# Stick-breaking attention: a block's products are issued after the next block's turnings, with more operand tiles, and the last keys' values are added by GpSimd

## The chip, the cores and the metric

The kernel runs on one core of one Trainium2 chip. The metric is the device time of one execution in microseconds (us), as the median of several runs. The core has five engines that matter here: PE (TensorE, matmuls; PEld is its weight load), DVE (VectorE), ACT (ScalarE), POOL (GpSimd) and SP (SyncE, which issues nearly all DMA transfers). PSUM is the memory that PE writes to, SBUF the one for operands.

## The reference, cut to what matters

The reference is one step of a two-layer encoder, width 1024, 16 heads of 64, with 2048 prompt frames and 64 sample frames that follow 2048 cached ones. Layer 0 (mixer A) attends in a band of chunks with softmax, layer 1 (mixer B) with stick-breaking:

```python
def sb_block(q, k, v, q_pos, k_pos):
    z = jnp.einsum('bqhd,bkhd->bhqk', q, k).astype(jnp.float32) * SCALE
    mask = (k_pos[None, :] < q_pos[:, None])[None, None]
    log_fail = jnp.where(mask, jax.nn.log_sigmoid(-z), 0.0)
    later = jnp.flip(jnp.cumsum(jnp.flip(log_fail, -1), axis=-1), -1) - log_fail
    w = jnp.where(mask, jnp.exp(jax.nn.log_sigmoid(z) + later), 0.0)
    return jnp.einsum('bhqk,bkhd->bqhd', w.astype(v.dtype), v)
```

So the weight of a key is its own sigmoid times the product of (1 − sigmoid) of all keys between it and the query. Both mixers multiply their result by SiLU(gate), project it and add it to the stream. A last normalization follows.

The kernel uses another form of the sum over keys: with the stick that is left, s, after each key, the weights are differences of neighbouring s. The sum of weight times value is then a sum of s times the difference of neighbouring values, and at the end one term is left over per query tile, the value of the tile's last key. That term is what `last_values` and `ends` hold.

## The kernel before, in words

The work stands in stages: mixer A's projections (0 to 776 us in the trace), the band attention with its output projection (776 to 1452), mixer B's projections of keys, values, queries and gate (1454 to 2083), the stick-breaking attention (about 2100 to 3347), and the rest of its output projection with the last normalization (to the end). The scheduler of the tile framework orders each engine's instructions by a timeline of its own; the order in which the program issues them gives a priority only.

In the stick-breaking stage the loops run over pairs of heads `hp` (8), groups of 512 queries `g` (4), the head `h` in the pair (2) and chunks of 512 keys `c`, from the diagonal backwards. An item is one such chunk. `scores` (L467) makes z on PE, with q as the standing operand. `pass_sticks` turns z into sticks: ACT makes f = sigmoid (L1008), POOL multiplies neighbours, `two` (L1019), DVE runs the cumulative product, a scan (L1021, or L1011 on the diagonal), and POOL fills the other half, s (L1024). Then `weigh` (L483 to L509) takes one pack of four 128x128 squares of s: `flip` (L128) turns them on PE into the PSUM tile `wt`, `split` (L135 to L137) cuts them into two operands, a high half `ph` (ACT, L136) and a low half `pl` (DVE, L137), and two products per block add `vt` times each half into the PSUM tile `acc` (L499). `ph` and `pl` have four tiles each. `weigh_sample` (L511 to L558) does the same for the 64 sample frames, with narrower tiles `pp` (L538).

The left-over term is a matmul too. In mixer B's projections `stage_ends` (L357 to L364) reads the last row of each 128 values, splits it and writes it to DRAM, `v_end`. At the start of the attention this is loaded into `last_values`, and POOL builds a table `upto` of 17 rows of ones at the right tiles (17 `affine_select`, 17 casts). The first pack of each `acc` then issues, between its high and its low product, `acc <- upto, last_values` (L509, 64 of 128x512; L547, 16 of 128x64 for the sample).

When the last chunk is done, `gate_out` (L470 to L481) joins the two halves of `acc`: ACT copies one (L477), DVE adds the other (L478), and for the second head POOL multiplies by the gate (L480) and SP writes the result `o`.

`pipelined` (L700 on) runs the items with a lag of one: the scores of one item are issued interleaved with the weighing of the item before, and between them pieces of `filler`, projection jobs for the next queries and gates (`ps_j`, L601 to L603) and the output projection (`ps_o`). 54 `ps_j` matmuls stand before the first scores of the stick-breaking stage. Queries go to DRAM in eight writes per job (`q_b`, L166) and come back by `load_q` (L399), keys by L412, values by L419, gates by L405, all on SP's queue.

Of the kernel before, what the change touches and what calls it, by code (L numbers as in the profile page):

```python
# [16 lines left out]
P = 128  # L17
# [52 lines left out]
def encoder_step(ctx: ExitStack, tc: tile.TileContext, a: dict, o: dict):  # L70
# [41 lines left out]
    vend = dram.tile([len(TOK), H, P], F32R, name="v_end")  # L112

# [16 lines left out]
    banks = {}  # L130
# [226 lines left out]
    def stage_ends(half, pool, psum):  # L357
        cols, heads, n = slice(half * CH, half * CH + CH), slice(half * 8, half * 8 + 8), len(TOK)
        cur = pool.tile([P, CH], F32, name="vcur", tag="vr", bufs=2)
        nc.sync.dma_start(cur[: n - 1], vraw[1 : 1 + NP, cols].rearrange("(t p) c -> t p c", p=P)[:, P - 1])  # L360
        nc.sync.dma_start(cur[n - 1 : n], vraw[T : T + 1, cols])
        vs = pool.tile([P, 8, 2, DH], F32R, name="vs", tag="vs", bufs=2)
        split(vs[:n, :, 0, :], vs[:n, :, 1, :], cur[:n].rearrange("p (h d) -> p h d", d=DH))
        nc.sync.dma_start(f32(vend[:, heads]), f32(vs[:n]).rearrange("p h s d -> p h (s d)"))  # L364

# [106 lines left out]
    def gate_out(L, pool, acc, h, c0, n, gt, ot, hp, g):  # L472

        lo, up = slice(0, DH), slice(DH, P)
        mine, other = (lo, up) if h == 0 else (up, lo)
        tmp = pool.tile([P, CH], F32, name="otmp", tag="otmp", bufs=1)
        nc.scalar.activation(tmp[mine, :n], acc[other, c0 : c0 + n], AF.Copy)  # L477
        nc.vector.tensor_tensor(ot[mine, :n], acc[mine, c0 : c0 + n], tmp[mine, :n], ALU.add)  # L478
        if h == 1:
            nc.gpsimd.tensor_tensor(ot[:, :n], ot[:, :n], gt[:, :n], ALU.mult)  # L480
            nc.sync.dma_start(lay[L]["o"][g][hp], ot[:, :n])  # L481

    def weigh(pool, psum, acc, blocks, first, last, ends=None):  # L483
# [11 lines left out]
        for s, part in enumerate((ph, pl)):  # L495
            at = 0
            for i, (ws, v, c0) in enumerate(blocks):
                m = len(ws) * P
                last_mm[0] = mm(  # L499
                    acc[:, c0 : c0 + m],  # L500
                    v,
                    part[:, at : at + m],
                    start=(first and s == 0 and i == 0),
                    stop=(last and s == 1 and i == len(blocks) - 1),
                    skip_group_check=True,
                )
                at += m
            if ends and s == 0:
                mm(acc, *ends, start=False, stop=False, skip_group_check=True)  # L509

    def weigh_sample(pool, psum, total, blocks, first, ends=None):  # L511
# [13 lines left out]
        for f in flips:  # L525
            f()
        acc = psum.tile([P, CH], F32, name="acc", tag="acc", bufs=1)
        for i, pack in enumerate(packs):

            pp = pool.tile([P, 2, 2, 2, NS], F32R, name="pp", tag="ph", bufs=4)  # L530
# [5 lines left out]
            for j, (_, _, v, _) in enumerate(pack):  # L536
                for h in range(2):
# [8 lines left out]
                    if ends and i == 0 and j == 0:  # L546
                        mm(acc[:, h * P : h * P + NS], *ends[h], start=False, stop=False, skip_group_check=True)  # L547
# [154 lines left out]
    def pipelined(items, lag, filler, more, ready, later, lead):  # L702
# [49 lines left out]
        for two in late:  # L752
            run([], two)

# [29 lines left out]
    staged_b = [partial(stage_ends, i) for i in range(2)]  # L784
# [20 lines left out]
    with (  # L805
# [6 lines left out]
        banks.update(wt=3, fo="wt")  # L812
# [46 lines left out]
        def item(hp, g, h, q, gt, ot, bias, keys, vs):  # L859
# [28 lines left out]
            def weigh_pack(i):  # L888
                if i == 0:
                    st["acc"] = psum.tile([P, CH], F32, name="acc", tag="acc", bufs=1)  # L890
                last = i == len(packs) - 1
                weigh(lpool, psum, st["acc"], [block(j) for j in packs[i]], i == 0, last)
                if last:
                    gate_out("a", lpool, st["acc"], h, 0, CH, gt, ot, hp, g)
# [61 lines left out]
    with (  # L956
# [17 lines left out]
        nc.vector.tensor_copy(own, own_s)  # L974

        last_values = wpool.tile([P, H, P], F32R, name="last_values")
        upto = wpool.tile([P, T], F32R, name="upto")
        nc.gpsimd.memset(f32(last_values), 0.0)
        nc.sync.dma_start(f32(last_values[: len(TOK)]), f32(vend))
        ones = pool.tile([P, CH + 1], F32, name="ones", tag="s", bufs=11)[:, :P]  # L980
        nc.gpsimd.memset(ones, 1.0)
        for t, (r0, n) in enumerate(TOK):
            row = pool.tile([P, CH], F32, name="row", tag="f", bufs=3)[:, :P]
            nc.gpsimd.affine_select(
                out=row, in_=ones, pattern=[[0, P]], compare_op=ALU.is_equal, fill=0.0, base=-t, channel_multiplier=1,
            )
            nc.gpsimd.tensor_copy(upto[:, r0 : r0 + n], row[:, :n])
        KV, SB = 4, 11
        banks.update(wt=4, fo="wt")
# [41 lines left out]
        def items():  # L1031
            for part in ORDER:
                yield sum(16 * (4 * g + 3) for g in part)
                for hp in range(HP):
                    kv = {}
                    for g in part:
                        for h in range(2):
                            q = load_q("b", pool, hp, h, g * CH)
                            acc = psum.tile([P, CH], F32, name="acc", tag="acc", bufs=1)
                            carry = {}  # L1040
                            for c in range(g, -1, -1):
# [5 lines left out]
                                yield item(hp, g, h, q, gt, ot, kv[c], acc, carry, c)  # L1047
# [5 lines left out]
        def item(hp, g, h, q, gt, ot, kv, acc, carry, c):  # L1053
# [109 lines left out]
```

## Time and profile before

| what | value |
|---|---|
| median of 3 runs | 3462.01 us (3460.86 to 3463.1) |
| profiled execution | 3459.85 us |
| its span | 3458.1 us |
| PE busy | 3304.3 us (96%) |
| PEld busy | 2811.4 us (81%) |
| DVE busy | 1920.0 us (56%) |
| ACT busy | 1661.0 us (48%) |
| POOL busy | 1176.0 us (34%) |

The span runs from the first to the last instruction of the profile. A row of a group reads: line, engine, operation, output <- inputs, the tile (standing rows*columns, then partitions x elements), xcount | busy us, mean ns of one | idle time of its engine just before these instructions, and what ended most of it. A row of a timeline reads: start, duration, engine, line, operation, xcount, and in brackets the idle time before it with its releaser. Matmuls on PE overlap one another, so two durations in a row may add to more than the time that they take.

### The profile page before, as it was taken

What the parts mean: (1) busy time and instruction counts of PE and PEld (TensorE: products, weight loads), DVE (VectorE), ACT (ScalarE), POOL (GpSimd) and SP (SyncE); (2) the same over time, 40 slices, a digit from 0 to 9 for tenths busy, and PEclk for the clock granted to TensorE, in tenths of its full rate; (3) what the DMA queues carried; (4) which work ended last, traced back from release to release, by engine and by line L of the source; (5) the groups of instructions that cost most, each with busy time, mean ns of one, the idle gap of its engine ahead of it and who ended that gap; (6) DMA issues with size and microseconds to landing.
All of it is one profiled execution on the core that took longest, in us unless ns stands there. A gap on an engine that the chain in (4) does not pass through costs nothing.

```text
span 3458.1 us, 53876 instructions
## 1 busy us (share of the span) xinstructions
PE 3304.3 (96%) x18064; PEld 2811.4 (81%) x18064; DVE 1920.0 (56%) x3863; ACT 1661.0 (48%) x3609; POOL 1176.0 (34%) x1845
## 2 busy tenths in 40 slices
PE   8999999999999999999999997999999998999999
PEld 6788999987887998787888996777777776777777
DVE  4224422118988883220233325877778888877763
ACT  5223322228887772141233324655656666655641
POOL 2001210005553340020233002333466667667650
PEclk9999999999999999999999999999999999999999
DMA  6349998257788755443699678665534454334333
GB/s 191 133 163 325 340 307 263 93 189 247 240 281 249 242 188 165 131 145 111 203 320 324 222 204 240 185 194 176 174 97 126 142 175 150 121 102 139 123 101 110
DMA packets 463906, 659.85 MB, mean 191 GB/s; under 512 B 53017, under 2 KB 272185, under 8 KB 463613
## 3 DMA queue, kind: packets, MB, share of 16 engines
q1 hardware_dynamic: 454094, 630.46, 57.6%
q10 hardware_dynamic: 9536, 25.96, 2.0%
q8 instruction: 143, 2.34, 0.3%
q14 instruction: 133, 1.09, 0.1%
HBM read 387.94 MB, written 268.34 MB: 190 GB/s over the span
## 4 chain that ended last, share of the span: by engine, by line
PE 63%; DMA 11%; DVE 11%; ACT 4%; issue 4%; SPq 4%; POOL 2%; ACTq 0%; DVEq 0%; POOLq 0%
PE acc L499 8%; PE z L467 6%; PE wt L128 6%; PE ps_t L156 5%; PE ps_t L157 5%; PE ps_t L155 5%; PE ps_v L157 4%; PE ps_v L155 4%; PE ps_v L156 4%; PE ps_o L692 3%; PE ps_o L693 3%; PE ps_o L694 3%; DVE pl L137 3%; DVE s L1011 2%; DVE s L1021 2%
## 5 line engine op out<-in xcount | busy, mean ns | idle before, releaser
L128 PE MATMUL wt<-ident,s 128*128 128x128 f32 (+1 forms) x3472 | 555.0, 275 | 24.1 <-DVE pl L137 6.5
L137 DVE TENSOR_TENSOR pl<-wt,ph 128x512 fp32r<-128x512 f32 (+1 forms) x864 | 540.5, 654 | 66.0 <-ACT ph L136 63.8
L136 ACT ACTIVATE ph<-wt 128x512 fp32r<-128x512 f32 (+1 forms) x864 | 464.6, 583 | 112.5 <-PE wt L128 97.2
L128 PEld LDWEIGHTS wt<-ident,s 128*128 128x128 f32 (+1 forms) x3472 | 417.9, 141 | 116.8 <-DVE pl L137 13.0
L1008 ACT ACTIVATE f<-z 128x512 f32<-128x512 f32 (+4 forms) x680 | 354.2, 543 | 298.0 <-PE z L467 148.6
L1024 POOL TENSOR_TENSOR s<-f,s 128x256 f32<-128x256 f32 x416 | 366.0, 881 | 169.9 <-DVE s L1021 164.7
L499 PE MATMUL acc<-pl,vt 128*128 128x512 f32 (+3 forms) x1088 | 365.9, 370 | 33.6 <-DVE pl L137 31.8
L467 PE MATMUL z<-kt,q 128*128 128x512 f32 (+3 forms) x1280 | 386.3, 395 | 11.8 <-ACT f L1008 9.4
L155 PE MATMUL ps_t<-x_own,wh 128*128 128x362 f32 (+1 forms) x1152 | 381.6, 331 | 3.0 <-ACT wh L141 3.0
L156 PE MATMUL ps_t<-x_own,wh 128*128 128x362 f32 (+1 forms) x1152 | 378.5, 329 | 0.0
L157 PE MATMUL ps_t<-x_own,wl 128*128 128x362 f32 (+1 forms) x1152 | 377.8, 328 | 0.0
L499 PE MATMUL acc<-ph,vt 128*128 128x512 f32 (+3 forms) x1088 | 354.8, 360 | 6.3 <-ACT ph L136 3.8
L831 POOL TENSOR_SCALAR s<-s,rc 128x640 f32<-128x640 f32 (+5 forms) x264 | 194.3, 743 | 488.5 <-DMA vt<-v_a 246.0
L1021 DVE TENSOR_TENSOR_SCAN s<-two,s,own 128x256 f32<-128x256 f32 x384 | 279.8, 739 | 73.1 <-POOL two L1019 71.9
L1019 POOL TENSOR_TENSOR two<-f 128x256 f32<-128x256 f32 x416 | 259.1, 628 | 112.5 <-ACT f L1008 110.9
L499 PEld LDWEIGHTS acc<-pl,vt 128*128 128x128 f32 x1088 | 193.6, 190 | 82.5 <-DVE pl L137 66.3
L499 PEld LDWEIGHTS acc<-ph,vt 128*128 128x128 f32 x1088 | 201.6, 189 | 44.0 <-ACT ph L136 15.8
L467 PEld LDWEIGHTS z<-kt,q 128*128 128x128 f32 x1280 | 201.5, 190 | 44.1 <-ACT f L1008 28.5
L155 PEld LDWEIGHTS ps_t<-x_own,wh 128*128 128x128 f32 x1152 | 218.1, 189 | 4.5 <-ACT wh L141 3.6
L1011 DVE TENSOR_TENSOR_SCAN s<-f,own 128x128 f32<-128x128 f32 (+4 forms) x264 | 201.5, 789 | 35.3 <-ACT f L1008 34.4
L156 PEld LDWEIGHTS ps_t<-x_own,wh 128*128 128x128 f32 x1152 | 218.4, 190 | 0.9
L157 PEld LDWEIGHTS ps_t<-x_own,wl 128*128 128x128 f32 x1152 | 218.0, 189 | 0.3
(155 smaller groups left out, 6379.1 us busy)
## 6 DMA issues: line engine op xcount, KB each, us to landing
vt<-v_b SPq DMA_DIRECT2D x80, 512.0 KB, 5.9
v_b<-vs SPq DMA_DIRECT2D x64, 512.0 KB, 5.5
q<-q_a SPq DMA_DIRECT2D x64, 512.0 KB, 4.1
q<-q_b SPq DMA_DIRECT2D x64, 512.0 KB, 4.2
vt<-v_a SPq DMA_DIRECT2D x48, 512.0 KB, 6.4
kt<-k_b SPq DMA_DIRECT2D x48, 512.0 KB, 6.3
keys<-k_a SPq DMA_DIRECT2D x40, 512.0 KB, 6.3
v_a<-vs ACTq DMA_DIRECT2D x32, 512.0 KB, 2.7
```

Of the source, the lines that this page charges most:

```text
L128: nc.tensor.transpose(out, in_, ident[: in_.shape[0], : in_.shape[0]])
L136: nc.scalar.activation(hi, src, AF.Copy)
L137: nc.vector.tensor_tensor(lo, src, f32(hi), ALU.subtract)
L155: mm(out, sh(k), mh(k), start=(k == 0), stop=False)
L156: mm(out, sh(k), ml(k), start=False, stop=False)
L157: mm(out, sl(k), mh(k), start=False, stop=(k == NK - 1))
L467: mm(z, q[:, i, t * P : t * P + P], kt[:, h], start=(i == 0), stop=(stop and i == 1), skip_group_check=not stop,)
L499: last_mm[0] = mm(acc[:, c0 : c0 + m], v, part[:, at : at + m], start=(first and s == 0 and i == 0), stop=(last and s == 1 and i == len(bl ...
L1008: nc.scalar.activation(f[:, x0:], z, AF.Sigmoid, scale=-SCALE)
L1011: nc.vector.tensor_tensor_scan(pr[:, rev], f[:, rev], own[:, rev], 1.0 if carry_in is None else carry_in, ALU.mult, ALU.max if diag else A ...
L1021: nc.vector.tensor_tensor_scan(pr[:, CH - 2 :: -2], two[:, ::-1], own[:, : CH // 2], carry_in, ALU.mult, ALU.bypass)
L1024: nc.gpsimd.tensor_tensor(pr[:, 1:CH:2], by2[:, :, 1], pr[:, 2 : CH + 1 : 2], ALU.mult)
```

## The change

Four things are changed together.

1. `weigh` and `weigh_sample` don't issue a block's products at once. `weigh` puts them into a list `held`, and the next `weigh` (or `weigh_sample`, or the end of `pipelined`) issues them after its own turnings and split. `acc` is allocated when the first products are issued, and `gate_out` follows the last ones. This holds for both mixers.
2. `ph` and `pl` have six tiles each in mixer B (four in mixer A, as before).
3. The matmuls `acc <- upto, last_values` are gone, and with them `stage_ends`, `v_end`, `last_values` and the table `upto`.
4. In their place a tile `ends["b"]` holds the last values by head pair and query tile. It is made at the start of the stick-breaking stage: four loads of rows of `v_raw` (16 rows and one row for each half of the width), eight turnings `ps_e` on PE, and two copies on ACT. `gate_out` then adds it, broadcast over 128 queries, to `ot` on POOL before the multiplication by the gate (32 of 128x512, 8 of 128x64).

```diff
-    def stage_ends(half, pool, psum):
-        cols, heads, n = slice(half * CH, half * CH + CH), slice(half * 8, half * 8 + 8), len(TOK)
-        cur = pool.tile([P, CH], F32, name="vcur", tag="vr", bufs=2)
...
-        nc.sync.dma_start(f32(vend[:, heads]), f32(vs[:n]).rearrange("p h s d -> p h (s d)"))
...
         if h == 1:
+            if L == "b":
+
+                t0, m = g * (CH // P), max(n // P, 1)
+                by = ot[:, :n].rearrange("p (t q) -> p t q", t=m)
+                last = ends["b"][:, hp, t0 : t0 + m].unsqueeze(2).to_broadcast([P, m, n // m])
+                nc.gpsimd.tensor_tensor(by, by, last, ALU.add)
             nc.gpsimd.tensor_tensor(ot[:, :n], ot[:, :n], gt[:, :n], ALU.mult)
...
+    held = []
+
+    def release():
+
+        while held:
+            held.pop(0)()
...
-        ph = pool.tile([P, CH], F32R, name="ph", tag="ph", bufs=4)
-        pl = pool.tile([P, CH], F32R, name="pl", tag="pl", bufs=4)
+        ph = pool.tile([P, CH], F32R, name="ph", tag="ph", bufs=banks["ph"])
+        pl = pool.tile([P, CH], F32R, name="pl", tag="pl", bufs=banks["ph"])
         split(ph[:, :n], pl[:, :n], wt[:, :n])
...
-            if ends and s == 0:
-                mm(acc, *ends, start=False, stop=False, skip_group_check=True)
...
+        def products():
+            to = acc()
...
+            then()
+
+        release()
+        held.append(products)
...
-    staged_b = [partial(stage_ends, i) for i in range(2)]
+    staged_b = []
...
-        nc.sync.dma_start(f32(last_values[: len(TOK)]), f32(vend))
...
+        ends["b"] = wpool.tile([P, HP, len(TOK)], F32, name="ends")
+        for half in range(2):
+            cols, n = slice(half * CH, half * CH + CH), len(TOK)
+            cur = pool.tile([P, CH + 1], F32, name="vcur", tag="s", bufs=SB)
+            nc.sync.dma_start(cur[: n - 1, :CH], vraw[1 : 1 + NP, cols].rearrange("(t p) c -> t p c", p=P)[:, P - 1])
+            nc.sync.dma_start(cur[n - 1 : n, :CH], vraw[T : T + 1, cols])
+            ps = psum.tile([P, CH], F32, name="ps_e", tag="wt", bufs=banks["wt"])
+            for j in range(4):
+                flip(ps[:, j * P : j * P + n], cur[:n, j * P : j * P + P])
+            nc.scalar.activation(
+                ends["b"][:, 4 * half : 4 * half + 4], ps.rearrange("p (j q) -> p j q", j=4)[:, :, :n], AF.Copy
+            )
```

**PE, the fourth pair of heads.** This is PE's order of before in the middle of the attention; the number behind a name tells tiles apart, and `wt_23555` is the tile whose halves are `ph_23560` and `pl_23561`.

```order
L128 MATMUL wt_23555<-ident_66,s_23525 128x128
L128 MATMUL wt_23579<-ident_66,s_23525 128x128
L128 MATMUL wt_23597<-ident_66,s_23525 128x128
...
L467 MATMUL z_23618<-kt_23257,q_23542 128x512 x2
L467 MATMUL z_23644<-kt_23257,q_23641 128x128 x2
L499 MATMUL acc_23357<-ph_23560,vt_23259 128x512
L499 MATMUL acc_23357<-pl_23561,vt_23259 128x512
L499 MATMUL acc_23357<-ph_23584,vt_23259 128x512
L128 MATMUL wt_23658<-ident_66,s_23551 128x128
L128 MATMUL wt_23658<-ident_66,s_23575 128x128
L128 MATMUL wt_23658<-ident_66,s_23593 128x128
```

And the same place after; here `wt_23485` belongs to `ph_23490` and `pl_23491`.

```order
L126 MATMUL wt_23485<-ident_66,s_23454 128x128
L126 MATMUL wt_23509<-ident_66,s_23454 128x128
L126 MATMUL wt_23527<-ident_66,s_23454 128x128
...
L456 MATMUL z_23548<-kt_23191,q_23473 128x512 x2
L456 MATMUL z_23568<-kt_23191,q_23566 128x128 x2
L504 MATMUL acc_23442<-ph_23490,vt_23193 128x512
L504 MATMUL acc_23442<-pl_23491,vt_23193 128x512
L504 MATMUL acc_23442<-ph_23514,vt_23193 128x512
L126 MATMUL wt_23582<-ident_66,s_23481 128x128
L126 MATMUL wt_23582<-ident_66,s_23505 128x128
L126 MATMUL wt_23582<-ident_66,s_23523 128x128
```

Nothing moved here: in both, the other blocks' last turnings, four turnings of a further tile (left out) and four matmuls of scores stand between a block's last turning and its first product.

**SP, the start of the stick-breaking stage.** Before, the first loads of queries, keys and values stand ahead of the eight writes of the last query job (`q_b_115`).

```order
L588 DMA lraw<-in_w_in_b 128x8x128
L399 DMA q<-q_b_108 128x2x512
L412 DMA kt<-k_b_116 128x2x512
L419 DMA vt<-v_b 128x4x256
L166 DMA q_b_115<-sh 64x1088 x4
L166 DMA q_b_115<-sl 64x1088 x4
L405 DMA gt<-gate_b_125 128x512
```

After, three of the new loads of `v_raw` rows stand there, and the fourth with the first loads behind the writes.

```order
L594 DMA lraw<-in_w_in_b 128x8x128
L994 DMA vcur<-v_raw 16x512
L995 DMA vcur<-v_raw 1x512
L994 DMA vcur<-v_raw 16x512
L164 DMA q_b_115<-sh 64x1088 x4
L164 DMA q_b_115<-sl 64x1088 x4
L995 DMA vcur<-v_raw 1x512
L388 DMA q<-q_b_108 128x2x512
L401 DMA kt<-k_b_116 128x2x512
```

On PE the eight turnings `ps_e` stand right behind the last projection matmul and ahead of the first `ps_j`, so that PE's next work waits for the fourth load.

**POOL, around one `gate_out`.** Before, at one head pair's `gate_out` in the stick-breaking stage:

```order
L1019 TENSOR_TENSOR two<-f 128x256
L1020 COPY s<-s 128x1
L1024 TENSOR_TENSOR s<-f,s 128x256
L1019 TENSOR_TENSOR two<-f 128x256
L480 TENSOR_TENSOR ot<-ot,gt 128x512
L1019 TENSOR_TENSOR two<-f 128x256
L1024 TENSOR_TENSOR s<-f,s 128x256 x2
```

After, at the `gate_out` in the same place of the sequence:

```order
L1031 TENSOR_TENSOR two<-f 128x256
L1032 COPY s<-s 128x1
L1036 TENSOR_TENSOR s<-f,s 128x256
L1031 TENSOR_TENSOR two<-f 128x256
L474 TENSOR_TENSOR ot<-ot,ends 128x512
L1031 TENSOR_TENSOR two<-f 128x256
L1036 TENSOR_TENSOR s<-f,s 128x256
L475 TENSOR_TENSOR ot<-ot,gt 128x512
L1036 TENSOR_TENSOR s<-f,s 128x256
```

The add stands where the multiplication stood, and the multiplication two instructions of the stick chain later.

More of the change, by code (lines that the diff above doesn't have):

```diff
@@ L888, in weigh_pack, with acc, then @@
             def weigh_pack(i):
[L889 to L890 removed]
+                def acc():
+                    if i == 0:
+                        st["acc"] = psum.tile([P, CH], F32, name="acc", tag="acc", bufs=1)
+                    return st["acc"]
+                def then():
+                    if last:
+                        gate_out("a", lpool, st["acc"], h, 0, CH, gt, ot, hp, g)
                 last = i == len(packs) - 1
[L892 to L894 removed]
+                weigh(lpool, psum, acc, [block(j) for j in packs[i]], i == 0, last, then)
             return [partial(tile_of, t) for t in range(4)], [partial(weigh_pack, i) for i in range(len(packs))]
@@ L974, in encoder_step @@
         nc.vector.tensor_copy(own, own_s)
-        last_values = wpool.tile([P, H, P], F32R, name="last_values")
-        upto = wpool.tile([P, T], F32R, name="upto")
-        nc.gpsimd.memset(f32(last_values), 0.0)
-        nc.sync.dma_start(f32(last_values[: len(TOK)]), f32(vend))
[L980 to L985, printed above, removed]
-            )
-            nc.gpsimd.tensor_copy(upto[:, r0 : r0 + n], row[:, :n])
-        KV, SB = 4, 11
-        banks.update(wt=4, fo="wt")
+        KV, SB = 4, 11
+        banks.update(wt=4, fo="wt", ph=6)
+        ends["b"] = wpool.tile([P, HP, len(TOK)], F32, name="ends")
[9 more added lines that the diff above has]
+                ends["b"][:, 4 * half : 4 * half + 4], ps.rearrange("p (j q) -> p j q", j=4)[:, :, :n], AF.Copy
+            )
         new = Sample("b", wpool)
@@ L1051, in items, with item @@
                     ready.append(GROUPS)
-        def item(hp, g, h, q, gt, ot, kv, acc, carry, c):
+        def item(hp, g, h, q, gt, ot, kv, sums, carry, c):
             tiles = []
@@ L1072, in weigh_pack, with acc, then @@
                 first = c == g and i == 0
-                ends = (last_values[:, 2 * hp + h], upto[:, g * CH : g * CH + CH]) if first else None
-                weigh(lpool, psum, acc, [block(j) for j in packs[i]], first, last, ends)
-                if last:
-                    gate_out("b", lpool, acc, h, 0, CH, gt, ot, hp, g)
+                def acc():
+                    if first:
+                        sums["acc"] = psum.tile([P, CH], F32, name="acc", tag="acc", bufs=1)
+                    return sums["acc"]
+                def then():
+                    if last:
+                        gate_out("b", lpool, sums["acc"], h, 0, CH, gt, ot, hp, g)
+                weigh(lpool, psum, acc, [block(j) for j in packs[i]], first, last, then)
             return [partial(tile_of, t) for t in range(4)], [partial(weigh_pack, i) for i in range(len(packs))]
@@ L1105, in two @@
             def two():
-                ends = [(last_values[:, 2 * hp + h], upto[:, NP:T]) for h in range(2)]
-                weigh_sample(lpool, psum, totals[hp], blocks, cs[0] == 4, ends if cs[0] == 4 else None)
+                weigh_sample(lpool, psum, totals[hp], blocks, cs[0] == 4)
                 if cs[-1] == 0:
```

49 lines of the change are left out of this document (21 added, 28 removed).

## The prediction

> **What bounds the kernel now.** I read the head of the page first, then the table of windows, then the groups of instructions by line, and last the timelines of the places that the change touches. The page's head gives the span and each engine's busy time:
>
> ```profile
> span 3458.1 us, 53876 instructions
> PE 3304.3 (96%) x18064; PEld 2811.4 (81%) x18064; DVE 1920.0 (56%) x3863; ACT 1661.0 (48%) x3609; POOL 1176.0 (34%) x1845
> ```
>
> TensorE (PE) is the bound on the average: 3458.1 − 3304.3 = 154 us is all that it idles. An average over stages isn't enough, so here are four windows of 100 us: the end of mixer B's projections, then the stick-breaking stage early, in the middle and late. The columns after the width are PE, PEld, DVE, ACT and POOL busy with their counts, then the granted clock, DMA share and GB/s.
>
> ```profile
> 2000.00:2100.00 100.00, 80.31 (x482) 79.23 (x480) 26.31 (x78) 24.05 (x75) 5.08 (x12) 0.92 0.78 216
> 2200.00:2300.00 100.00, 94.25 (x537) 78.41 (x535) 79.06 (x143) 58.34 (x135) 36.83 (x62) 1.00 0.65 189
> 2900.00:3000.00 100.00, 94.21 (x505) 72.64 (x503) 78.11 (x127) 58.81 (x120) 66.24 (x121) 1.00 0.40 126
> 3200.00:3300.00 100.00, 96.57 (x541) 77.46 (x540) 81.29 (x131) 62.73 (x126) 69.75 (x126) 1.00 0.40 127
> ```
>
> In the stick-breaking stage PE works 94 to 97% of the time, DVE about 80% and POOL up to 70%. So a matmul taken out there is worth nearly its own time, and PE's waits are worth at most 3 to 6%. Only one window shows a large hole, the first; I come to it below. Which waits does the hold aim at? The groups of the turning (L128), the split (L137) and the products (L499), with idle time before them and what ended it:
>
> ```profile
> L128 PE MATMUL wt<-ident,s 128*128 128x128 f32 x3456 | 552.3, 275 | 23.7 <-DVE pl L137 6.5 <-POOL s L1024 4.9 <-DVE pp L137 3.1
> L499 PE MATMUL acc<-pl,vt 128*128 128x512 f32 (+3 forms) x1088 | 365.9, 370 | 33.6 <-DVE pl L137 31.8
> L499 PEld LDWEIGHTS acc<-pl,vt 128*128 128x128 f32 x1088 | 193.6, 190 | 82.5 <-DVE pl L137 66.3
> ```
>
> Products wait 33.6 us on PE itself for the low half `pl`, and its weight load waits 66.3 us, of which most lies beside other matmuls. So the most that a perfect hold could bring is between 32 and 66 us.
>
> **The change, part by part.** *The matmuls removed.* Here are all 64 plus 16 instructions, and a place of each kind in PE's timeline.
>
> ```profile
> L509 PE MATMUL acc<-upto,last_values x64: 388/392/403, 2127.3 to 3333.2; 128*128 128x512 f32 x64
> L547 PE MATMUL acc<-upto,last_values x16: 297/297/298, 2170.5 to 2493.6; 128*128 128x64 f32 x16
> ```
>
> ```profile
> 2607.01 0.48 PE L499 MATMUL acc<-ph,vt 128*128 128x512 f32 x1
> 2607.32 0.39 PE L509 MATMUL acc<-upto,last_values 128*128 128x512 f32 x1
> 2607.55 0.40 PE L499 MATMUL acc<-pl,vt 128*128 128x512 f32 x1
> ```
>
> ```profile
> 2170.28 0.33 PE L538 MATMUL acc<-pp,vt 64*128 64x128 f32 x1 [0.26 <-DVE ot L478]
> 2170.53 0.30 PE L547 MATMUL acc<-upto,last_values 128*128 128x64 f32 x1
> 2170.76 0.32 PE L538 MATMUL acc<-pp,vt 64*128 64x128 f32 x1
> 2171.02 0.30 PE L547 MATMUL acc<-upto,last_values 128*128 128x64 f32 x1
> 2171.15 1.09 PE L538 MATMUL acc<-pp,vt 128*128 128x128 f32 x8
> ```
>
> Matmuls overlap, so the price is start to start and not the duration: 2607.55 − 2607.32 = 0.23 us for the wide one, 64 × 0.23 = 14.7 us. The narrow ones stand between products of the sample: from 2170.28 to 2171.15 two products and two of ours take 0.87 us; two products of 1.09 / 8 = 0.14 us alone would take 0.27, so ours cost 0.60 / 2 = 0.30 us, or up to 0.32 us where the weight loads bind; I take 0.32: 16 × 0.32 = 5.1 us. Together 19.8 us of PE time, on an engine that is 94 to 97% busy there. If PE instead waits in their place, part of it isn't seen: lower bound half, 10 us.
>
> *The hold.* As written, a block's products are issued after the next block's turnings. But the scheduler decides the order on PE, and the order of before has that already: between a block's turnings and its products there stand scores and products of others. The two orders, laid beside each other in the section on the change, show the same sequence at the same place. Over the 648 packs of the stick-breaking stage, the work on PE between the last turning and the first product, with each matmul at the trace's start-to-start time, has a median of 3618 ns before and 3450 ns after; in most packs that lose distance it is one removed matmul's. Where such a product does wait, distance isn't the reason:
>
> ```profile
> 2283.18 0.45 PE L499 MATMUL acc<-ph,vt 128*128 128x512 f32 x1
> 2285.11 0.50 PE L499 MATMUL acc<-pl,vt 128*128 128x512 f32 x1 [1.49 <-DVE pl L137]
> ```
>
> ```profile
> 2282.96 1.52 DVE L1011 TENSOR_TENSOR_SCAN s<-f,own 128x256 f32<-128x256 f32 x2
> 2284.40 2.45 DVE L137 TENSOR_TENSOR pl<-wt,ph 128x512 fp32r<-128x512 f32 x4
> ```
>
> DVE had two scans of 1.52 us ahead of the `pl` that PE wanted. Neither a hold nor six operand tiles in place of four shorten DVE's own queue. I cost the hold, the extra tiles and the small reordering together at 0, between −10 (a third of the 32 us) and +10 (giving each pack the mean wait that packs at its distance have in the trace, an estimate, the waits of products rise from 76 to 83 us).
>
> *The start of the stick-breaking stage.* The stage that made `v_end` in mixer B's projections is gone; in its place four loads of rows of `v_raw` and eight turnings `ps_e` stand between the last projection matmul and the first `ps_j`. That is the hole of the first window. PE, then SyncE's queue (SPq), then the landing of a 32 KB load of the same kind:
>
> ```profile
> 2083.03 0.32 PE L157 MATMUL ps_t<-x_own,wl 128*128 128x362 f32 x1
> 2100.54 0.79 PE L601 MATMUL ps_j<-big,lwh 128*128 128x512 f32 x1 [17.19 <-DVE sl L137]
> ```
>
> ```profile
> 2092.80 0.94 SPq L588 DMA_DIRECT2D lraw<-in_w_in_b  x1
> 2093.84 1.43 SPq L399 DMA_DIRECT2D q<-q_b  x1
> 2099.61 3.58 SPq L166 DMA_DIRECT2D q_b<-sh  x4
> 2103.29 3.84 SPq L166 DMA_DIRECT2D q_b<-sl  x4
> ```
>
> ```profile
> vcur<-v_raw SPq DMA_DIRECT2D x2, 32.0 KB, 2.0
> ```
>
> In the new order three of the four loads go out before the eight writes of `q_b`, and the fourth (one row) behind them. The writes end at 2103.29 + 3.84 = 2107.1; the load issues in about 0.4 us, lands some 2.0 us later at 2109.5, and after four turnings at the clock of an idle PE `ps_j` starts at 2110.5, not at 2100.54: +10 us. The first loads of q, keys and values move from 2093.84 to behind 2107.5, still before the 54 `ps_j` matmuls are through, and two waits at the stage's start, which were on loads, should shrink, since PE comes later and the loads come only some 3 us later:
>
> ```profile
> 2123.44 1.22 PE L467 MATMUL z<-kt,q 128*128 128x512 f32 x4 [2.61 <-ACT f L1008]
> 2138.73 0.41 PE L467 MATMUL z<-kt,q 128*128 128x128 f32 x2 [0.91 <-DMA q<-q_b]
> ```
>
> (ACT is named for the first; the chain of waits has a key load there.) They give back about 3 us. Net +7 us, bounds +4 (the last row lands faster) and +11 (nothing given back).
>
> *The adds on POOL.* 32 of 128x512 and 8 of 128x64, in front of the multiplication by the gate. The first row is the nearest, the same kind of operation on the same tile; then come VectorE's sum of two halves, and the stick chain's scan and `two`:
>
> ```profile
> L480 POOL TENSOR_TENSOR ot<-ot,gt 128x512 f32<-128x512 f32 x64 | 82.7, 1292 | 133.4 <-DVE ot L478 124.4 <-DMA gt<-gate_a 8.9
> L478 DVE TENSOR_TENSOR ot<-acc,otmp 64x512 f32<-64x512 f32 x128 | 87.7, 685 | 68.5 <-ACT otmp L477 66.6
> L1021 DVE TENSOR_TENSOR_SCAN s<-two,s,own 128x256 f32<-128x256 f32 x384 | 279.8, 739 | 73.1 <-POOL two L1019 71.9
> L1019 POOL TENSOR_TENSOR two<-f 128x256 f32<-128x256 f32 x416 | 259.1, 628 | 112.5 <-ACT f L1008 110.9
> ```
>
> 32 × 1.29 = 41 us of POOL time, on an engine with 30 to 60% of its time free in this stage. Behind an add on POOL stand the next `two` and `s` of the stick chain, and DVE's scans wait for `two`; PE itself waited on POOL's `s` for 4.9 us only (the L128 row above). One block's scores are a whole item ahead of its products, which covers a delay of 1.3 us in most places. Bounds 0 and 41 us; nearest is the 4.9 us over 416 `s`, so I take +3, range 0 to 8. The 17 selections and 17 casts of the removed table stood on POOL where it is 5% busy (first window): 0.
>
> A rule of the Trainium skill speaks against this part: GPSIMD Engine Reference, section 4.1, gives elementwise sums of two tiles to VectorE, with GpSimd about twice as slow. The trace agrees (1292 ns here; VectorE's sum of half the partitions at L478 has a mean of 685 ns), and by VectorE the sum would be 32 × 0.69 = 22 us on the engine that is already late for `pl`. So row and rule lead apart, and POOL, which PE rarely waits for, is the cheaper place here.
>
> *Mixer B's projections.* Two `stage_ends` with six DMAs go from SyncE's queue, where the first row stood ahead of PE's first wait there, the second row:
>
> ```profile
> 1669.81 7.48 SPq L344 DMA_DIRECT2D vcur<-v_raw  x2
> 1695.24 0.93 PE L128 MATMUL ps_n<-ident,kf 128*128 128x128 f32 x4 [2.17 <-ACT kn L386]
> ```
>
> Of these 2.17 us and the smaller waits behind them I take −2, bounds −4 and +4 (another order on the queue can also cost a wait of this size). Mixer A keeps its instructions and four tiles, and its order changes slightly: 0, in the ±10 above.
>
> *The sum.* −19.8 + 0 + 7 + 3 − 2 = −11.8, rounded to −11 for what PE's remaining waits take up. The profiled execution took 3459.85 us (span 3458.1 and 1.75 around it), so it would take about 3449; the median of the runs is 2.2 us higher, 3462.01, and the forecast for the median is **3451 us**.
>
> **The rivals.**
>
> *The hold does what it says.* If products really wait behind more work, most of the `pl` waits go: 32 to 66 us, say 40, so 3451 − 40 = 3411 us. For it: `pl` is the largest releaser of PE. Against it: the order on PE barely moves, and DVE, 80% busy, is what is late. Chance 0.10.
>
> *Nothing is left of it.* The removed matmuls only filled waits (half of 19.8 = 10 us remains), the start costs 10 or 11 and POOL 0 to 8: −10 + 10 + 3 − 2 = +1 at one end, and −4 with 5 of the start given back: 3458 to 3463 us. For it: POOL and DVE both show gaps that PE's order doesn't control. Against it: PE at 94 to 97%. Chance 0.23.
>
> *POOL becomes late, slower.* If each add stands just before a `two` or `s` for which scan, flips and so PE wait, all 41 us come onto the path: 3451 − 3 + 41 = 3489 us. It decides from about 15 us, when the adds eat the 19.8 + 2 − 7 of the other terms, and from 22 us it can be measured. For it: DVE idles 71.9 us on `two`, and POOL works 66 to 70% late in the stage. Against it: PE's own 4.9 us on `s`. Chance 0.07.
>
> The same end could be reached by another way, a block of VectorE by GpSimd. These rows are DVE's subtractions between 2199 and 3300 us, min/median/max in ns:
>
> ```profile
> L137 DVE TENSOR_TENSOR pl<-wt,ph x516: 398/679/694, 2199.6 to 3299.0; 128x512 fp32r<-128x512 f32 x155, 128x256 fp32r<-128x256 f32 x17
> L137 DVE TENSOR_TENSOR big<-woraw,big x16: 656/693/1371, 2831.7 to 2911.1; 128x512 fp32r<-128x512 f32 x16
> ```
>
> `pl`, with one operand in PSUM, never took over 694 ns in 516; `big`, with both in SBUF, took up to 1371. Only such subtractions would be hit by the adds, and they are few: under 1 us in all. The Trainium skill, SBUF — State Buffer, in "SBUF: two separate sides", says that VectorE with two SBUF inputs and GpSimd lock a port pair against each other; the trace agrees in these two rows.
>
> **How the numbers follow.** Forecast 0.60, nothing left 0.23, hold works 0.10, POOL late 0.07. A measurement of this kernel can tell about 0.2%, or 6.9 us: faster is under 3455.1, slower over 3468.9. The forecast's own range is 3443 to 3459 (the bounds −10 and +10 taken less than fully, with the others), of which about a fifth lies over 3455: faster 0.48 + 0.10 + 0.03 of the second case = 0.61; same 0.12 + 0.19 = 0.31; slower 0.07 + 0.01 = 0.08. The range reaches from 3440 (nearly the lower bound of the reordering) to 3463 (the second case), and leaves out the hold's and POOL's cases, 0.17.
>
> **What would show it.** PE's busy time falls by 64 × 0.39 + 16 × 0.30 = 30 us as the page counts it; the groups L509 and L547 are gone. The idle time before products for `pl` stays between 25 and 40 us; under 15 would prove the hold right and me wrong. From the last projection matmul to the first `ps_j` it is 17.5 us before (2100.54 − 2083.03) and should be 26 to 29; under 21 would prove the start's term wrong. The add takes about 1.29 us each, and the flips' wait on POOL's `s` stays under 13 us; 30 or more would be the slower rival.

## The result and the profile after

The changed kernel takes 3477.63 us in the median of 4 runs (3473.66 to 3482.18), the kernel before in the same comparison 3461.44 us (4 runs, 3457.29 to 3463.1). The ratio is 1.0054 with a 95% interval from 1.0040 to 1.0067: 18.7 us slower, where 3451 us and a range to 3463 had been forecast. The profiled execution took 3478.49 us with a span of 3476.7 us. Below, a difference between two runs is the difference of their ratios to the kernel before, times 3460 us; a ratio's interval is about ±0.001, so a single difference carries some ±5 us.

The head of the page after, and its groups of turnings, products and scans:

```profile
span 3476.7 us, 53697 instructions
PE 3291.9 (95%) x17992; PEld 2800.0 (81%) x17992; DVE 1922.3 (55%) x3861; ACT 1655.6 (48%) x3609; POOL 1200.7 (35%) x1849
```

```profile
L126 PE MATMUL wt<-ident,s 128*128 128x128 f32 x3456 | 559.8, 276 | 36.3 <-POOL s L1036 10.3 <-DVE pp L135 6.7 <-DVE s L1023 4.4
L504 PE MATMUL acc<-pl,vt 128*128 128x512 f32 (+3 forms) x1088 | 366.4, 370 | 42.2 <-DVE pl L135 39.7
L474 POOL TENSOR_TENSOR ot<-ot,ends 128x512 f32<-128x512 f32 x32 | 33.4, 1043 | 85.0 <-DVE ot L467 84.8
L1033 DVE TENSOR_TENSOR_SCAN s<-two,s,own 128x256 f32<-128x256 f32 x384 | 280.4, 738 | 94.6 <-POOL two L1031 93.3
```

PE is busy for 12 us less and the span is 18.6 us longer: PE idles 185 us, not 154. Its waits before the `pl` products didn't go with the hold, they rose from 33.6 us to 42.2; the waits before turnings rose from 23.7 to 36.3 us, and DVE's scans wait 93.3 us for POOL's `two`, where it was 71.9. PE's busy time isn't a pure count of work: the same 17,992 matmuls of the changed kernel and its variants were busy for 3280.3 us in the trace with the highest mean granted clock (0.994, run `early_six_tiles`) and for 3294.1 us in one at 0.990 (`early_ends`). The changed kernel's trace has 0.989, that of the kernel before 0.991. How much of a difference in time is a difference in clock, no run separates.

The windows of 1210 us inside the stick-breaking stage show the same from PE's side, the kernel before first and the changed one second:

```profile
2130.00:3340.00 1210.00, 1148.99 (x6322) 921.00 (x6320) 972.35 (x1623) 739.14 (x1563) 706.03 (x1276) 1.00 0.48 145
```

```profile
2130.00:3340.00 1210.00, 1128.09 (x6208) 899.92 (x6206) 964.92 (x1615) 730.53 (x1557) 733.01 (x1301) 1.00 0.48 145
```

PE idles 1210 − 1148.99 = 61.0 us before and 81.9 us after. The windows stand at fixed times, while the stage begins later after the change, so here are the same two traces cut at events: the last projection matmul, the stage's first scores, and the last product.

| part | before, us | PE idle | after, us | PE idle |
|---|---|---|---|---|
| all before the last projection matmul | 2083.0 | 63.2 | 2084.0 | 62.9 |
| to the first scores | 32.0 | 17.2 | 44.4 | 28.1 |
| first scores to last product | 1245.1 | 65.4 | 1244.5 | 85.9 |
| behind the last product | 98.0 | 8.1 | 103.8 | 7.9 |

The stick-breaking stage is as long as before, although 80 matmuls are gone from it: what was taken from PE there came back as waiting. The start costs 12.4 us, and the work behind the last product takes 5.8 us more. Ahead of the stage little changes in sum, but two parts of it do: from its first scores to its last product mixer A's band attention takes 4.6 us more (536.2 and 540.8), and mixer B's projections take 4.5 us less (632.0 and 627.5).

The start of the stage, on PE and on SP's queue:

```profile
2083.99 0.32 PE L155 MATMUL ps_t<-x_own,wl 128*128 128x362 f32 x1
2102.77 0.58 PE L126 MATMUL ps_e<-ident,vcur 17*128 17x17 f32 x4 [18.45 <-DVE sl L135]
2113.00 0.58 PE L126 MATMUL ps_e<-ident,vcur 17*128 17x17 f32 x4 [9.65 <-DMA vcur<-v_raw]
2113.50 0.79 PE L607 MATMUL ps_j<-big,lwh 128*128 128x512 f32 x1
```

```profile
2097.59 0.30 SPq L994 DMA_DIRECT2D vcur<-v_raw  x1
2101.80 3.11 SPq L164 DMA_DIRECT2D q_b<-sh  x4
2105.01 4.35 SPq L164 DMA_DIRECT2D q_b<-sl  x4
2109.40 1.19 SPq L995 DMA_DIRECT2D vcur<-v_raw  x1
```

This is the chain that the prediction described: the fourth load is issued behind the eight writes, PE's second four turnings wait 9.65 us for it, and the first `ps_j` comes 2113.50 − 2083.99 = 29.5 us after the last projection matmul. The two waits of 2.61 and 0.91 us that the prediction expected to shrink are gone from the start of the stage.

### The profile page after: what moved, and what is told of

It reads as the page before. It is cut to its first block, busy times and chain, and to the rows that moved or that the text cites. A ratio compares the mean times of both kernels' runs of the same rounds, so it can differ in the third digit from the quotient of the medians.

```text
span 3476.7 us, 53697 instructions
## 1 busy us (share of the span) xinstructions
PE 3291.9 (95%) x17992; PEld 2800.0 (81%) x17992; DVE 1922.3 (55%) x3861; ACT 1655.6 (48%) x3609; POOL 1200.7 (35%) x1849
## 4 chain that ended last, share of the span: by engine, by line
PE 46%; DVE 13%; DMA 6%; issue 4%; ACT 4%; POOL 3%; SPq 2%; ACTq 0%; DVEq 0%; POOLq 0%
PE acc L504 7%; PE z L456 6%; PE wt L126 5%; DVE pl L135 4%; PE ps_o L698 3%; PE ps_o L699 3%; PE ps_o L700 3%; DVE s L1023 3%; DVE s L1033 3%; PE ps_v L153 2%; PE ps_v L155 2%; PE ps_v L154 2%; PE ps_j L607 2%; PE ps_t L154 2%; PE ps_t L155 2%
## 5 line engine op out<-in xcount | busy, mean ns | idle before, releaser
L126 PE MATMUL wt<-ident,s 128*128 128x128 f32 (+1 forms) x3472 | 562.8, 276 | 36.3 <-POOL s L1036 10.3
L504 PE MATMUL acc<-pl,vt 128*128 128x512 f32 (+3 forms) x1088 | 366.4, 370 | 42.2 <-DVE pl L135 39.7
L456 PE MATMUL z<-kt,q 128*128 128x512 f32 (+3 forms) x1280 | 384.7, 395 | 14.5 <-ACT f L1020 12.6
L1033 DVE TENSOR_TENSOR_SCAN s<-two,s,own 128x256 f32<-128x256 f32 x384 | 280.4, 738 | 94.6 <-POOL two L1031 93.3
L504 PEld LDWEIGHTS acc<-pl,vt 128*128 128x128 f32 x1088 | 193.7, 190 | 89.3 <-DVE pl L135 73.4
L504 PEld LDWEIGHTS acc<-ph,vt 128*128 128x128 f32 x1088 | 201.5, 190 | 44.4 <-ACT ph L134 15.5
L349 POOL TENSOR_TENSOR vprev<-vprev,vcur 128x512 f32<-128x512 f32 (+1 forms) x66 | 86.7, 1313 | 410.3 <-DMA vprev<-in_cache_b_v 150.7
```

What stands on the lines that cost most here:

```text
L126: nc.tensor.transpose(out, in_, ident[: in_.shape[0], : in_.shape[0]])
L456: mm(z, q[:, i, t * P : t * P + P], kt[:, h], start=(i == 0), stop=(stop and i == 1), skip_group_check=not stop,)
L504: last_mm[0] = mm(to[:, c0 : c0 + m], v, part[:, at : at + m], start=(first and s == 0 and i == 0), stop=(last and s == 1 and i == len(blo ...
L1033: nc.vector.tensor_tensor_scan(pr[:, CH - 2 :: -2], two[:, ::-1], own[:, : CH // 2], carry_in, ALU.mult, ALU.bypass)
```

## The experiments

All runs were made in five rounds beside the kernel before, each round on another chip; so runs are compared by their ratios. Three theories were set against each other: the hold costs; the adds on POOL cost; the changed order of instructions gives changes of any sign.

**The parts undone one at a time.** First the hold:

```diff
-        release()
-        held.append(products)
+        products()
```

> The changed kernel with the hold undone: each block's products are issued right behind its own turnings and split, everything else as changed (six tiles, adds on POOL, new start). If the hold costs, by the trace after: mixer A's band took 685 us after against 679 before (6 us), and PE's waits in the stick-breaking stage grew by some 20 us, of which the hold would have half. Theory 'hold' expects 10 to 16 us less than the changed kernel (ratio to before about 1.001 to 1.003). Theory 'POOL' expects only the 6 us of mixer A (ratio about 1.004). A rival, that any rearrangement of the order gives changes of this size, expects no rule: either sign, up to 10 us.

Measured: 3468.82 us, ratio 1.0033 (1.0021 to 1.0045). 7 us less than the changed kernel: below the 10 to 16 that 'hold' expected, close to the 6 that 'POOL' allowed, and not outside the rival of either sign up to 10 us. This run alone doesn't tell the theories apart.

The hold alone was put into the kernel before (the list `held` and the late `acc`, with the matmuls of the last values inside the held products).

> The kernel before with the hold alone, four tiles, its matmuls of the last values kept inside the held products. Theory 'hold' expects 10 to 16 us more than before (3471 to 3477, ratio 1.003 to 1.005), 6 of it in mixer A's band. Theory 'POOL' expects no more than those 6 us (ratio up to 1.002).

Measured: 3462.72 us, ratio 1.0011 (1.0001 to 1.0021), 4 us. Less than 'hold' expected, and within what 'POOL' allowed. In its trace the stick-breaking stage, cut at events as above, was no longer than before (1243.4 and 1245.1 us), and the band attention was (540.6 and 536.2 us).

The changed kernel without the adds:

```diff
-                nc.gpsimd.tensor_tensor(by, by, last, ALU.add)
```

> The changed kernel without the 40 adds on POOL; the last keys' values are left out of mixer B's result, the tile for them is still made. Theory 'POOL': DVE's wait on POOL's two rose from 78 to 97 us and PE's wait on POOL's s from 4.9 to 8.7 us, so the adds' 33 us of POOL time lie partly on the stick chain: 12 to 20 us less than the changed kernel. Theory 'hold' expects 0 to 5 us less.

Measured: 3464.6 us, ratio 1.0016 (1.0006 to 1.0027), 13 us less. As 'POOL' expected.

The table of last values made in mixer B's projections, through memory, and read back in one load:

```diff
-    staged_b = []
+    staged_b = [partial(stage_ends, i) for i in range(2)]
...
+        nc.sync.dma_start(ends["b"], endsd)
```

> The changed kernel with the table of last values made in mixer B's projections (turned there, written to memory, and read back in one load at the start of the stick-breaking stage), so that no turning stands between the last projection matmul and the first ps_j. In the trace after, this gap is 29.6 us (2083.99 to about 2113.6) against 17.5 before. All theories expect the gap to go back to 17 to 18 us; of the 12 us, 8 to 12 us should show in the time, since the later start gave back at most a few us at the first key loads.

Measured: 3465.31 us, ratio 1.0026 (1.0015 to 1.0037), 9.7 us less, as expected.

The six tiles back to four:

```diff
-        banks.update(wt=4, fo="wt", ph=6)
+        banks.update(wt=4, fo="wt", ph=4)
```

> The changed kernel with four operand tiles in place of six in mixer B. The prediction gave the tiles nothing: within 4 us of the changed kernel (ratio to before 1.0054, give or take 0.0012). If the hold needs them, so that a held pack would block the next split, 5 to 15 us more.

Measured: 3468.6 us, ratio 1.0035 (1.0022 to 1.0049). Some 6.6 us less and not more; the held packs don't need the two tiles. The intervals of this run and the changed kernel overlap a little.

**The matmuls and the adds, in the kernel before.** The 80 matmuls alone were left out:

```diff
-            if ends and s == 0:
-                mm(acc, *ends, start=False, stop=False, skip_group_check=True)
...
-                    if ends and i == 0 and j == 0:
-                        mm(acc[:, h * P : h * P + NS], *ends[h], start=False, stop=False, skip_group_check=True)
```

> The kernel before without the 80 matmuls of the last values; the last keys' values are left out of mixer B's result, and the tables for them are still loaded and built. The prediction's term: 64 x 0.23 + 16 x 0.32 = 19.8 us less than before (ratio 0.9943). The rival that the first runs point to (no_add, which has the start's 10 us and the hold as well, is only 5.5 us over before): PE waits in part of their place, so only 8 to 12 us less (ratio 0.9965 to 0.998).

Measured: 3447.83 us, ratio 0.9968 (0.9957 to 0.9979): 11 us less, not 19.8. The rival's number.

The adds alone:

```diff
+            if L == "b":
+                m = max(n // P, 1)
+                by = ot[:, :n].rearrange("p (t q) -> p t q", t=m)
+                nc.gpsimd.tensor_tensor(by, by, nhalf.unsqueeze(2).to_broadcast([P, m, n // m]), ALU.add)
```

> The kernel before with 40 more adds on POOL in gate_out of mixer B, in front of the multiplication by the gate, of a constant -0.5 broadcast over the tile, so that the result is off by that; nothing else is changed. Leaving out the adds took 13 us off the changed kernel. If the price is POOL's time on the stick chain, 10 to 15 us more than before (ratio 1.003 to 1.0045). If it came only from the changed kernel's own order, -5 to +5 us.

Measured: 3458.61 us, ratio 1.0002 (0.9993 to 1.0011): nothing. This went against the theory 'POOL' as it stood: the same adds that cost 13 us in the changed kernel cost nothing here. Either the changed kernel's order was to blame, or the removed matmuls had covered the adds. The next runs ask that: both edits together, without hold, tiles or a new start.

> The kernel before without the 80 matmuls and with 40 adds on POOL in their place (of a constant -0.5, so that mixer B's result is off); no hold, four tiles, start as before. Theory 'cover' (the stick chain over POOL and DVE is nearly as long as PE's work; the adds lengthen the chain, and PE's matmuls hid that): the 11 us of the removal and the 13 us of the adds cancel, -3 to +5 us against before (ratio 0.999 to 1.0015). Theory 'additive' (adds cost nothing, as add_only showed; the changed kernel's rest is order): -8 to -14 us (ratio 0.996 to 0.9977).

Measured: 3455.21 us, ratio 0.9997 (0.9988 to 1.0006): 1 us less than before. −11 and +0.7 don't add to −1; without the matmuls the adds cost 10 us. And with a second add per `gate_out`, with all matmuls kept:

> The kernel before with all its matmuls and 80 adds on POOL (two per gate_out, of a constant, result off). Theory 'cover': the cover ends somewhere, so the second add costs what the first did not, 5 to 15 us more than before (ratio 1.0015 to 1.0045). Theory 'additive': again nothing, within 3 us.

Measured: 3473.76 us, ratio 1.0047 (1.0035 to 1.0060): 16 us, just over the expected range. And without the matmuls:

> The kernel before without the 80 matmuls and with 80 adds on POOL (result off). Theory 'cover': another 10 to 20 us over swap_only. Theory 'additive': the same as swap_only within 3 us.

Measured: 3467.62 us, ratio 1.0026 (1.0015 to 1.0038): 10 us over `swap_only`. Four runs as 'cover' has it: the first add is free beside the matmuls and costs 10 us without them, the second costs 10 to 16 us in either.

The windows of 1210 us again: no matmuls, adds alone, both, two adds beside the matmuls, and two adds without them:

```profile
2130.00:3340.00 1210.00, 1141.77 (x6286) 914.64 (x6285) 973.52 (x1630) 739.68 (x1565) 714.06 (x1275) 1.00 0.48 146
```

```profile
2130.00:3340.00 1210.00, 1147.17 (x6331) 922.19 (x6329) 970.67 (x1624) 740.90 (x1564) 743.53 (x1313) 1.00 0.48 146
```

```profile
2130.00:3340.00 1210.00, 1136.39 (x6256) 906.71 (x6256) 974.78 (x1626) 740.46 (x1568) 745.94 (x1315) 1.00 0.48 146
```

```profile
2130.00:3340.00 1210.00, 1138.25 (x6248) 907.70 (x6247) 963.81 (x1607) 731.41 (x1548) 763.52 (x1335) 1.00 0.48 145
```

```profile
2130.00:3340.00 1210.00, 1136.57 (x6212) 902.40 (x6211) 974.07 (x1614) 733.43 (x1553) 769.30 (x1345) 0.99 0.48 145
```

PE idles 68.2, 62.8, 73.6, 71.8 and 73.4 us in them, against 61.0. From the first scores to the last product it idles 69.9, 66.3, 77.5, 75.9 and 80.1 us, against 65.4. Without the matmuls it waits 4.5 to 7 us more. With the adds beside the matmuls it waits only 1 to 2 us more, and with either the matmuls gone too or a second add, 11 to 13 us more. The last of the five doesn't follow: its second add costs 10 us in time and at most 3 us of further waits; PE is busy 14.5 us longer than in `swap_only` for the same 17,984 matmuls, at a mean granted clock of 0.989 against 0.993. So for the first add PE's waits go with the times, and for the second without the matmuls a lower clock is a rival that no run rules out. DVE's wait for `two` is 71.9 us before, 86.5 with one add and 72.7 with two, so it doesn't carry this reading. That POOL's part of the stick chain is what PE then waits for is the likely way, not shown step by step.

**What is left: hold, tiles, start.** The changed kernel without hold and with four tiles:

> The changed kernel without the hold and with four tiles: what is left is the swap of matmuls for adds and the new start. If the parts add up as measured apart (swap -1 us, start +10), 9 us over before (ratio 1.0026, 1.0013 to 1.004). If the hold or the six tiles carry more than the 4 to 7 us seen so far (the sum of the parts is 4 to 5 us short of the changed kernel's 18.7), it comes out at 1.002 or less; if neither matters, at 1.004 or more.

Measured: 3462.43 us, ratio 1.0004 (0.9994 to 1.0015): 1 us over before, not 9. So hold and tiles together make up 17 us of the 18.7. With the early table as well, so that the swap is left, with its true values (and with the later place of `acc` in the program):

> The same with the table of last values made in mixer B's projections, so that only the swap is left, with the true values. By swap_only (ratio 0.9997) it should be within 4 us of before. If the place where the table is made costs time of its own in the projections, 4 to 10 us more.

Measured: 3454.32 us, ratio 0.9983 (0.9974 to 0.9993): 6 us less than before. This version, which leaves nothing out, beats both kernels. In its trace PE's gap at the start is 18.7 us, close to the 17.5 of before:

```profile
2075.94 0.32 PE L156 MATMUL ps_t<-x_own,wl 128*128 128x362 f32 x1
2094.68 0.79 PE L619 MATMUL ps_j<-big,lwh 128*128 128x512 f32 x1 [18.42 <-DVE sl L136]
```

The late table costs 1.0004 − 0.9983, 7 us without the hold, and 9.7 us with it.

From this version the hold was put back in mixer A alone, in mixer B alone, and the six tiles without a hold:

```diff
+        if banks["wt"] == 3:
+            release()
+            held.append(products)
+        else:
+            products()
```

> The early table with four tiles, and the hold in mixer A alone. In the traces of kernels with the hold, the band attention has 82 to 84 us of PE waits, in those without it 76 to 82; one place stands out, where ACT's split of output weights waits for its load ahead of the sample's split and PE waits 2.3 to 4.0 us more. If this is the hold's price in mixer A: 4 to 6 us over the early table without hold (0.9983), a ratio of 0.9993 to 1.0003. If mixer A's part is only one trace's spread: 0.9983 again.

Measured: 3455.89 us, ratio 0.9999 (0.9989 to 1.0008), 5.5 us over the version without.

> The early table with four tiles, and the hold in mixer B alone. The two traces with four tiles and late table differ by 6 us of PE waits in the stick-breaking stage (199.5 with the hold, 193.4 without): a ratio of 0.9998 to 1.0008. If the hold's price lies in mixer A only: 0.9983.

Measured: 3455.87 us, ratio 0.9999 (0.9990 to 1.0007), also 5.5 us.

> The early table without the hold, with six operand tiles. By the times with the late table (1.0033 with six, 1.0004 with four) 10 us over 0.9983, a ratio of 1.001. By the traces (PE's waits 196.4 and 193.4 us in the stage) only 3 us, a ratio of 0.999. If tiles cost nothing: 0.9983.

Measured: 3454.85 us, ratio 0.9992 (0.9984 to 1.0001), 3 us, which is inside the interval of nothing. Each of the three differences is about as large as its own error. Their sum of 14 us agrees with the two runs that have all three or none beside the early table: `early_ends` at 1.0026 against 0.9983, 15 us.

In mixer A the price can be seen at one place. ACT's timeline with the hold in mixer A, and in the run with the hold in mixer B alone:

```profile
1030.15 0.63 ACT L135 ACTIVATE big<-woraw 128x512 fp32r<-128x512 f32 x1 [4.29 <-DMA woraw<-in_w_out_a]
1030.69 0.36 ACT L135 ACTIVATE pp<-wt 128x256 fp32r<-128x256 f32 x1
```

```profile
1025.47 0.38 ACT L135 ACTIVATE pp<-wt 128x256 fp32r<-128x256 f32 x1 [0.48 <-PE wt L127]
1026.57 0.37 ACT L135 ACTIVATE pp<-wt 128x256 fp32r<-128x256 f32 x1
1028.40 0.25 ACT L135 ACTIVATE pp<-wt 64x128 fp32r<-64x128 f32 x1
1028.79 0.63 ACT L135 ACTIVATE big<-woraw 128x512 fp32r<-128x512 f32 x1
```

With the hold, the split of a piece of output weights stands ahead of the sample's split on ACT; ACT waits 4.29 us for that piece's load, and the sample's `pp` waits behind it. PE's timeline with the hold in mixer A, and the changed kernel's:

```profile
1031.98 1.42 PE L127 MATMUL wt<-ident,s 128*128 128x128 f32 x6 [3.24 <-DVE pp L136]
```

```profile
1032.14 1.10 PE L126 MATMUL wt<-ident,s 128*128 128x128 f32 x6 [3.85 <-DVE pp L135]
```

Without the hold, PE has no such wait there. The traces of all 19 kernels bear this out: in the six with the hold in mixer A, PE waits 1.9 to 4.6 us at this place, in the other thirteen no wait between 1010 and 1045 us is over 1.3 us. From its first scores to its last product the band attention takes 538.1 to 541.8 us in the six and 534.2 to 538.2 us in the thirteen, 4.3 us apart in the mean. So one instruction that changed places on ACT explains most of mixer A's part.

In mixer B no single place stands out. From the stage's first scores to the end of the execution the hold adds 4.6 to 12.9 us in the four pairs of traces without the matmuls of the last values, and takes 1.7 us less in the one pair with them (`hold_only`). So here too the price seems to depend on the matmuls that are gone. The waits for `pl` aren't the way: by the page's groups they go from 34.4 to 36.1 us with the hold in mixer B, and to 39.4 us with six tiles in place of four, though the tiles cost less time there. Which wait begins the loss stays open.

**The adds on other engines.** Two versions had the early table, no hold and four tiles, as the version that beats both kernels, and added the values elsewhere. On ACT, as a bias of its copy:

> A version meant to be faster: the changed kernel without the hold, four tiles, the table of last values made in mixer B's projections, and the last values added by ACT as the bias of its copy in gate_out (four copies of 64x128 with a bias in place of one of 64x512), not by POOL. From the runs so far: 18.7 over before, minus 7 for the hold, 10 for the start, 13 for the adds = 11 us less than before, plus the cost on ACT: the small copies take some 0.29 us each by the sigmoid of 128x128, so 64 x (4 x 0.29 - 0.59) = 36 us of ACT time, which is 58% busy and releases PE and DVE; 0 to 15 us of it on the path. So between -11 and +4 us against before (ratio 0.997 to 1.001).

Measured: 3461.37 us, ratio 1.0010 (1.0000 to 1.0020), the upper end of the expected. On DVE, within its sum:

> A version meant to be faster: the changed kernel without the hold, four tiles, the table made in mixer B's projections, and the last values added by DVE within its sum of the two halves in gate_out (four of 64x128 with a value per partition in place of one of 64x512). Estimated DVE cost: small DVE operations took 0.15 (one column) to 0.32 us (64x64), so four take about 1.3 us against 0.685, 64 x 0.6 = 38 us on DVE, which is 80% busy and the last releaser of products. Without matmuls, hold, start and POOL adds the removal alone gave -11 us; with DVE's share on the path, -8 to +8 us against before (ratio 0.9977 to 1.0023).

Measured: 3458.3 us, ratio 0.9999 (0.9989 to 1.0008). Both are slower than the add on POOL (0.9983), by 9 and 5.5 us, the second of them hardly beyond its error. On DVE four sums with a value per partition stand in place of one of 0.685 us; one of the four takes 0.347 us, but they overlap, and four in a row took 1.12 and 1.17 us at two places. DVE's busy time rose by 23 us (1921.1 to 1944.0) and POOL's fell by 34 us (1201.3 to 1167.1), and still the kernel was no faster. The Trainium skill gives an elementwise sum to VectorE (GPSIMD Engine Reference, section 4.1). Here the sum on the less loaded POOL was at least as good, though DVE did it in four pieces and not as one sum, so the rule itself isn't tested.

## Why the prediction was wrong, point by point

**The hold and the tiles: 0 forecast, 17 us measured.** This is the step that failed. The prediction had shown that the sequence of turnings and products at a place of mixer B doesn't move, which is right, and inferred that the order is as good as before. In mixer A, which it gave "0, in the ±10 above", the price lies in what else the scheduler moved when priorities changed: one split on ACT went ahead of another and waited for a load, 4 to 5.5 us. In mixer B the hold costs 5.5 us by the runs and the tiles 3 to 10, and which wait carries them stays open. The order for the hold was compared on PE, at the place that the edit names, and not on ACT and DVE. The bound of +10 was too near for a hold in two mixers and a larger pool.

**The removed matmuls: −19.8 forecast, −11 measured.** The PE time was right (PE busy fell by 3304.3 − 3285.9 = 18.4 us in that run); the forecast of 30 us "as the page counts it" was not, since overlapping matmuls aren't counted twice. But about 9 us of the 19.8 were lost, and 4.5 to 7 us can be seen as waits in the stage. The lower bound of 10 us, given in the text and used only by a rival, was the answer.

**The adds: +3 forecast, 0 to +13 measured.** With the matmuls there they cost nothing; with them gone, 10 us, and 13 us in the changed kernel. The two terms were summed as if apart, and they aren't: the first add is free only beside the matmuls. PE's 4.9 us of waiting on `s` was not the nearest row, since it was measured with the matmuls in place. One add took 1.04 us, not 1.29.

**The start: +7 forecast, +7 to +10 measured.** Right, with the mechanism. The gap is 29.5 us, just over the forecast 26 to 29; the last load took 2113.00 − 2109.40 = 3.6 us from its issue to PE, not 2.4.

**Mixer B's projections: −2 forecast.** In the traces the stretch from mixer A's last output matmul to the last projection matmul takes 625.6 to 627.5 us in the five kernels with the late table and 625.0 to 633.6 us, 630.2 in the mean, in the seven with the old one. That is 3 to 4 us less, and fits. The step from the swap with a constant (0.9997) to the fastest version (0.9983), −5 us with an error as large, isn't the same: that version has a `stage_ends` of its own, and only the splits, the load of `v_end` and the table on POOL are gone.

Read as steps from before to after, the runs give −11 (matmuls), +10 (adds), −5 (old table gone), +7 (late start), +17 (hold and tiles), in sum 18, against 18.7 measured. Each step starts at the kernel where the last one ended, so the sum has to come out but for rounding, and it proves nothing about a single step. Of the rivals, 'nothing is left of it' had the right reason for the first two, and none had a cost of the hold.

Of the signs that the prediction named, two stayed within what it set although its time was wrong: the waits of products for `pl` (39.7 us, up to 40 allowed) and of turnings for POOL's `s` (10.3 us, under 13). They were set for whole rivals and couldn't show a loss spread over several waits. The threshold of 22 us for the slower rival is 21 by its own sum (3451 − 3 + 21 = 3469).

## What to carry to other kernels

In a stage where PE works 95% of the time and its feeding chain is nearly as long, a matmul taken out and an operation put on the chain can't be priced apart: here 11 of 19.8 us were left of the first, and one add per `gate_out` was free only as long as the first was there. And an edit to the program's order under a scheduler has to be compared on every engine's queue and in every stage that shares the code, above all for instructions that wait on a load and now stand ahead of others; that the edited sequence itself is unchanged says little.

## What the runs showed of the hardware

The add on POOL with a broadcast operand (L474 above) took 1043 ns for 128x512, where the product of two full tiles takes 1292 ns. The operation isn't the reason, as the changed kernel also adds two full tiles on POOL, in its projections:

```profile
L289 POOL TENSOR_TENSOR kf<-sh,sl 128x512 f32<-128x512 f32 x38 | 49.5, 1304 | 84.4 <-DVE sl L135 75.8 <-DMA k_b<-kh 3.4 <-PE ps_n L126 1.9
```

So a sum with one value read for 128 columns took a fifth less time than a sum of two full tiles.
